# The last two output blocks of the second feed-forward cut at 384 tokens instead of 256

## Chip, cores and metric

One core of a Trainium2 chip runs the whole block, forward pass only, for one sequence of 512 tokens. The metric is the time of one execution in device microseconds; three timed runs of the kernel before and one profiled execution are at hand.

## What is computed

The input x is 512 tokens of 1024 channels. The block has a first feed-forward, a token mixer (an mLSTM branch and a gated delta-net branch, with gates and an output projection), a second feed-forward and a last RMS norm. The change is in the second feed-forward and the norm behind it:

```python
def swiglu(h, w_in, w_out):
    gate, up = jnp.split(h @ w_in, 2, axis=-1)
    return (jax.nn.silu(gate) * up) @ w_out
...
        h = modulate(rms_norm(x, norm_ffn2[l]), mod[:, 2, 0], mod[:, 2, 1])
        x = x + FFN_RES * mod[:, 2, 2][:, None, :] * swiglu(h, w_ffn2_in[l], w_ffn2_out[l])
    return rms_norm(x, norm_final)
```

D_MODEL is 1024 (eight tiles of 128 channels, KO = 8), D_FF is 2816 (22 tiles of 128, in two halves of HJ = 11). All inputs are float32.

## The kernel before

Activations lie with channels on the 128 partitions and tokens along the free axis, so a tile of 128 channels is 128x512. Every large product is made of three matmuls: weights and activations are each split into a rounded high part and a rest (`whi`, `wlo`; `acth`, `actl`; all of the type fp32r), and `mm3` adds high times high, high times low and low times high into one PSUM bank. The weights are the stationary operand (128 columns), the activations the moving one. Small products, those of the norm among them, are plain float32 and appear in the trace as two records each.

`ffn` (the second one is called in the last line of the kernel's main function, L1303) works in two halves of the hidden tiles. Behind each half come the output blocks: `out_block(o, ...)` multiplies 11 weight tiles with 11 hidden tiles into one bank, 33 matmuls, then VectorE adds the result to x (L388), and in the second half ScalarE squares x (L295, tile `sq`, for the last block `sqlast`) and VectorE sums the squares over the blocks (L297, `sqacc`). In the second half the blocks 0 to 5 are done for all 512 tokens. The last two, 6 and 7, are done in two token ranges: both blocks for the first range, then `norm` for that range, then both for the second range, then `norm` for it. Their two weight tiles are held for both ranges.

For the second feed-forward, `norm` is `final` (L1293). It calls `rms_bcast`: per group of 128 tokens, a product of `sqacc` and one of `sqlast` with a column of ones gives the sums over channels (tile `psm`), VectorE makes the mean square (L306, L309), GpSimd raises it to the power -1/2 (L312, `rr`), and one product per group of 128 tokens spreads it over the partitions (`psm<-cstt,rr`). ScalarE scales x by the norm's weight (L1297), and VectorE multiplies by the spread value, two channel tiles at a time (L1299); behind each such step SyncE issues a DMA of the two tiles to HBM (L1301), four per token range.

The order on each engine is set by a scheduler from the order of the program, so that matmuls of the second range stand between the steps of the first range's norm. The queues themselves are served in order. `pbig` is the bank of an output block (three of them in turn).

Of the kernel before, what the change touches and what calls it, by code (L numbers as in the profile page):

```python
# [17 lines left out]
P = 128  # L18
S = 512
TB = S // P  # L20
# [145 lines left out]
def hybrid_block(ctx: ExitStack, tc: tile.TileContext, I, outT, dbg=None, upto=99):  # L166
# [13 lines left out]
    def big():  # L180
        b = ps.tile([P, S], F32, tag="big", name="pbig", bufs=3)
        return b

    def st2():
        b = ps.tile([P, S], F32, tag="st", name="pst", bufs=2)
        return b

    def sm():
        b = ps.tile([P, S], F32, tag="sm", name="psm", bufs=3)
        return b  # L190
# [9 lines left out]
    x = p1.tile([P, KO, S], F32, name="x")  # L200
# [23 lines left out]
    def wtile(src, n=2048, lo=vec):  # L224
        raw = wraw(src, n)
        hi = W.tile([P, 2048], F32R, tag="whi", name="whi")
        wl = W.tile([P, 2048], F32R, tag="wlo", name="wlo")
        for c in range(0, n, 1024):
            e = slice(c, min(n, c + 1024))
            act.activation(hi[:, e], raw[:, e], AF.Copy)  # L230
            lo.tensor_tensor(out=wl[:, e], in0=raw[:, e], in1=hi[:, e].bitcast(F32), op=ALU.subtract)  # L231
        return hi, wl

    def wk(src, c=256, lo=vec):
        hi, lo = wtile(src, KO * c, lo)
        return (hi[:, :KO * c].rearrange("p (k c) -> p k c", c=c),
                lo[:, :KO * c].rearrange("p (k c) -> p k c", c=c))

    def mm3(o, wh, wl, xh, xl, n=KO):
        for k in range(n):  # L240
            mm(o, wh(k), xh(k), start=(k == 0), stop=False)
            mm(o, wh(k), xl(k), start=False, stop=False)
            mm(o, wl(k), xh(k), start=False, stop=(k == n - 1))
# [4 lines left out]
    ghalf = cst.tile([P, 16], F32, name="ghalf")  # L248
# [39 lines left out]
    ALL = (slice(0, S), range(TB))  # L288
    HALVES = ((slice(0, S // 2), range(TB // 2)), (slice(S // 2, S), range(TB // 2, TB)))

    def sumsq(x, k, sq, tp, c=ALL[0], fold=False):
        if c.start == 0:
            tag = "sqacc" if k == 0 else "sqlast" if k == KO - 1 else "sq"
            sq[k] = tp.tile([P, S], F32, tag=tag, name=tag, bufs=2 if tag == "sq" else 1)
        act.activation(sq[k][:, c], x[:, k, c], AF.Square)  # L295
        if 0 < k < (KO if fold else KO - 1):
            vec.tensor_tensor(out=sq[0][:, c], in0=sq[0][:, c], in1=sq[k][:, c], op=ALU.add)  # L297
# [20 lines left out]
    def new_h():  # L318
        hh = Hp.tile([P, KO, S], F32R, tag="hh", name="hh")
        hl = Hp.tile([P, KO, S], F32R, tag="hl", name="hl")  # L320
        return hh, hl

    def split(dst_h, dst_l, src):
        act.activation(dst_h, src, AF.Copy)
        vec.tensor_tensor(out=dst_l, in0=src, in1=dst_h.bitcast(F32), op=ALU.subtract)
# [19 lines left out]
        return f  # L345


    def ffn(x, hh, hl, gcol, wi, wo, tp, norm, side=(), pre=(), first=(ALL,), store=None):
        side, pre = list(side), list(pre)
        sq = {}  # L350
        for half in range(2):
            ah, al = [], []
            for jj in range(HJ):
                j = half * HJ + jj
                if j == 0 and not pre:
                    w0 = [wk(wi[i]) for i in range(2)]
                    p0 = [(big(), big()), (st2(), st2())]
                    for c, _ in first:
                        for (wh, wl), pp in zip(w0, p0):
                            for o, c0 in zip(pp, (0, P)):  # L360
                                mm3(o[:, c], lambda k: wh[:, k, c0:c0 + P], lambda k: wl[:, k, c0:c0 + P],
                                    lambda k: hh[:, k, c], lambda k: hl[:, k, c])
                if j < len(pre):
                    pg, pu = pre[j]
                elif j < 2:
                    pg, pu = p0[j]
                else:
                    wh, wl = wk(wi[j - len(pre)])
                    pg, pu = big(), big()
                    for o, c0 in ((pg, 0), (pu, P)):  # L370
                        mm3(o, lambda k: wh[:, k, c0:c0 + P], lambda k: wl[:, k, c0:c0 + P],
                            lambda k: hh[:, k], lambda k: hl[:, k])
                sg = tp.tile([P, S], F32, tag="sg", name="sg", bufs=2)
                act.activation(sg, pg, AF.Silu)  # L374
                vec.tensor_tensor(out=sg, in0=sg, in1=pu, op=ALU.mult)  # L375
                a_h = tp.tile([P, S], F32R, tag="acth", name="acth", bufs=HJ + 2)
                a_l = tp.tile([P, S], F32R, tag="actl", name="actl", bufs=HJ + 2)
                split(a_h, a_l, sg)
                ah.append(a_h)
                al.append(a_l)  # L380
                if side and j > 1:
                    side.pop(0)()

            def out_block(o, wh, wl, c):
                po = big()
                mm3(po[:, c], lambda k: wh[:, k * P:(k + 1) * P], lambda k: wl[:, k * P:(k + 1) * P],
                    lambda k: ah[k][:, c], lambda k: al[k][:, c], n=HJ)
                vec.scalar_tensor_tensor(out=x[:, o, c], in0=po[:, c], scalar=gcol[:, o:o + 1], in1=x[:, o, c],  # L388
                                         op0=ALU.mult, op1=ALU.add)
                if half == 1:  # L390
                    sumsq(x, o, sq, tp, c)
                    if store is not None and c.stop == S:
                        nc.sync.dma_start(store[:, o], x[:, o])

            for o in range(KO - 2 * half):
                out_block(o, *wtile(wo[o, half], HJ * P), ALL[0])
                if half == 0 and side:
                    side.pop(0)()
        w2 = [wtile(wo[o, 1], HJ * P) for o in (KO - 2, KO - 1)]
        for c, ts in HALVES:  # L400
            for o, w in zip((KO - 2, KO - 1), w2):
                out_block(o, *w, c)
            norm(sq, c, ts)
        assert not side, len(side)
# [38 lines left out]
    hh, hl = new_h()  # L443
    pre = [(big(), big()), (big(), st2()), (st2(), sm()), (sm(), sm())]
    for k in range(KO):
# [36 lines left out]
    negm = cst.tile([P, 2, P], BF16, name="negm")  # L482
    hm = []
    ffn(x, hh, hl, ghalf[:, 0:8], I["wi1"], I["wo1"], pa1, norm_mod(x, 1, hm, p1),
        [lambda b=b, q=q: ada(b, q, pa1) for b in (2, 4, 3, 5, 7, 6, 8) for q in range(4)], pre, store=xd)
    hh, hl = hm
# [144 lines left out]
    for t in range(TB):  # L631
        ts = slice(t * P, (t + 1) * P)
# [16 lines left out]
    for t in range(TB - 1, -1, -1):  # L649
        ts = slice(t * P, (t + 1) * P)  # L650
# [75 lines left out]
    for h in range(H):  # L726
        wh, wl = wk(I["wmqk"][h])
        qk = []
        for i in range(2):
            pq = big()  # L730
            c = slice(i * P, (i + 1) * P)
# [17 lines left out]
        for t in range(TB):  # L749
            ts = slice(t * P, (t + 1) * P)  # L750
# [18 lines left out]
        for t in range(TB):  # L769
            ts = slice(t * P, (t + 1) * P)  # L770
# [39 lines left out]
    for h2 in range(4):  # L810
        wh, wl = wk(I["wmo"][h2])
        for i in range(2):
            h = h2 * 2 + i
            c = slice(i * P, (i + 1) * P)
# [66 lines left out]
    for h in range(H):  # L881
        if h % 2 == 0:
            wvh, wvl = wk(I["wgv"][h // 2])
            for i in range(2):
                c = slice(i * P, (i + 1) * P)
# [7 lines left out]
        for i in range(2):  # L893
            c = slice(i * P, (i + 1) * P)
# [33 lines left out]
        for d in range(2):  # L928
# [4 lines left out]
            for t in range(TB):  # L933
                for hf in range(2):
                    c = slice(t * P + hf * 64, t * P + hf * 64 + 64)
# [3 lines left out]
        for c2 in range(2):  # L939
            pk = st2()  # L940
            for cc in range(2):
                t = c2 * 2 + cc
                ts = slice(t * P, (t + 1) * P)
# [221 lines left out]
    for pr in range(H // 2):  # L1165
        hs = (2 * pr, 2 * pr + 1)
        L = {}
        for h in hs:
            tp = g3c if pr % 2 else g3a
# [9 lines left out]
        for n in range(TB):  # L1179
            rrs, banks = {}, {}  # L1180
            for ci, (h, d) in enumerate(chains):
                vt, X, kd, kq, A, xst, ost = L[h]
                t = n if d == 0 else TB - 1 - n
                ts = slice(t * P, (t + 1) * P)
# [17 lines left out]
            for h, d in chains:  # L1202
                vt, X, kd, kq, A, xst, ost = L[h]
                t = n if d == 0 else TB - 1 - n
                ts = slice(t * P, (t + 1) * P)
# [62 lines left out]
    x = px.tile([P, KO, S], F32, name="x2")  # L1268
    nc.sync.dma_start(x, xd)
    hm = []  # L1270
# [20 lines left out]
    p2 = Lines(ctx.enter_context(tc.tile_pool(name="p2", bufs=1)))  # L1291

    def final(sq, c, ts):  # L1293
# [4 lines left out]
        for k in range(0, KO, 2):  # L1298
            vec.tensor_tensor(out=x[:, k:k + 2, c], in0=x[:, k:k + 2, c],  # L1299
                              in1=rb[:, c].unsqueeze(1).to_broadcast([P, 2, n]), op=ALU.mult)  # L1300
            nc.sync.dma_start(outT[:, k:k + 2, c], x[:, k:k + 2, c])  # L1301

    ffn(x, hm[0], hm[1], ghalf[:, 8:16], I["wi2"], I["wo2"], p2, final, first=HALVES)  # L1303


# [17 lines left out]
```

## Time and profile before

| what | value |
|---|---|
| timed runs | 1569.15, 1570.06, 1571.91 us (median 1570.06) |
| profiled execution, its own time | 1564.87 us |
| its span in the trace | 1563.1 us |
| mean granted TensorE clock | 0.995 |
| TensorE matmul busy | 1529.7 us, 98% of the span |
| VectorE, ScalarE busy | 860.5 us (55%), 731.1 us (47%) |

The profiled execution lies 5.2 us below the median of the timed runs, and its span 1.8 us below its own time. Matmuls are pipelined and their ends are modelled, so the cadence of a matmul is read from the starts of many in a row and not from its duration.

### The profile page before, as it was taken

The numbers are of one execution on the slowest core, as the hardware profiler recorded it, in microseconds if no ns is written. First come the engines' busy times: TensorE is split into PE (matmuls) and PEld (weight loads), VectorE is DVE, ScalarE is ACT, GpSimd is POOL, SyncE is SP. The second block draws the span as 40 slices with busy tenths as digits, with TensorE's granted clock in tenths as the row PEclk, the third lists the DMA queues.
The fourth block names the chain that finished last, engine by engine and source line by source line (L and its number), as shares of the span: only waits on it lengthen the run. The fifth ranks groups of instructions, "written<-read, shape, count | busy, mean of one in ns | idle before, by whom it ended". The sixth has DMA issues, their size and how long they took to land.

```text
span 1563.1 us, 20823 instructions
## 1 busy us (share of the span) xinstructions
PE 1529.7 (98%) x7920; PEld 1288.6 (82%) x7920; DVE 860.5 (55%) x1577; ACT 731.1 (47%) x1654; POOL 54.7 (4%) x88
## 2 busy tenths in 40 slices
PE   8999999999999999989999999989999999999997
PEld 6888888888788888768888887879889888888887
DVE  7897843335735555657677683347556323332333
ACT  4422223223447757886666536757434322222232
POOL 0000000000000000021121200000000000000000
PEclk9999999999999999999999999999999999999999
DMA  9687832233332231364565766675531322323222
GB/s 362 224 335 281 299 139 96 75 113 113 116 133 95 81 95 55 121 212 173 188 205 174 257 243 196 194 290 173 192 136 55 110 98 74 110 108 108 70 88 73
DMA packets 75014, 244.50 MB, mean 156 GB/s; under 512 B 23937, under 2 KB 26369, under 8 KB 58402
## 3 DMA queue, kind: packets, MB, share of 16 engines
q1 hardware_dynamic: 74914, 243.17, 44.7%
q8 instruction: 62, 1.02, 0.3%
q14 instruction: 38, 0.31, 0.1%
HBM read 207.43 MB, written 35.72 MB: 156 GB/s over the span
## 4 chain that ended last, share of the span: by engine, by line
PE 92%; ACT 3%; DVE 2%; DMA 2%; issue 1%; SPq 0%; POOL 0%; POOLq 0%; DVEq 0%; ACTq 0%
PE pbig L193 76%; PE pst L193 8%; PE psm L193 7%; DMA L<-grd 1%; DMA kd<-kdd 0%; PE pst L876 0%; ACT L L936 0%; ACT whi L230 0%; DMA xtd<-X 0%; PE pst L1158 0%; PE pst L909 0%; DVE cmx L645 0%; PE pst L747 0%; ACT L936 0%; PE psm L823 0%
## 5 line engine op out<-in xcount | busy, mean ns | idle before, releaser
L193 PE MATMUL pbig<-hh,whi 128*128 128x512 f32 (+1 forms) x1304 | 509.4, 392 | 7.2 <-ACT whi L230 5.6
L193 PE MATMUL pbig<-hl,whi 128*128 128x512 f32 (+1 forms) x1304 | 507.6, 390 | 0.0
L193 PE MATMUL pbig<-hh,wlo 128*128 128x512 f32 (+1 forms) x1304 | 507.6, 390 | 0.0
L230 ACT ACTIVATE whi<-raw 128x1024 fp32r<-128x1024 f32 (+1 forms) x249 | 237.1, 985 | 421.4 <-PE pbig L193 349.9
L231 DVE TENSOR_TENSOR wlo<-raw,whi 128x1024 fp32r<-128x1024 f32 (+1 forms) x249 | 278.3, 1137 | 99.1 <-ACT whi L230 94.2
L193 PEld LDWEIGHTS pbig<-hh,whi 128*128 128x128 f32 x1304 | 245.5, 189 | 54.3 <-ACT whi L230 5.8
L193 PEld LDWEIGHTS pbig<-hh,wlo 128*128 128x128 f32 x1304 | 245.8, 189 | 49.3 <-DVE wlo L231 1.1
L193 PEld LDWEIGHTS pbig<-hl,whi 128*128 128x128 f32 x1304 | 246.0, 189 | 47.9
L375 DVE TENSOR_TENSOR sg<-sg,pbig 128x512 f32<-128x512 f32 x40 | 27.5, 688 | 233.7 <-PE pbig L193 233.7
L193 PE MATMUL pbig<-acth,whi 128*128 128x512 f32 (+1 forms) x396 | 145.2, 367 | 0.0
L193 PE MATMUL pbig<-acth,wlo 128*128 128x512 f32 (+1 forms) x396 | 144.7, 365 | 0.0
L193 PE MATMUL pbig<-actl,whi 128*128 128x512 f32 (+1 forms) x396 | 144.7, 365 | 0.0
L193 PEld LDWEIGHTS pbig<-actl,whi 128*128 128x128 f32 x396 | 74.7, 189 | 12.1
L193 PEld LDWEIGHTS pbig<-acth,whi 128*128 128x128 f32 x396 | 74.7, 189 | 12.1
L193 PEld LDWEIGHTS pbig<-acth,wlo 128*128 128x128 f32 x396 | 74.6, 188 | 12.1
L374 ACT ACTIVATE sg<-pbig 128x512 f32<-128x512 f32 x41 | 24.6, 599 | 124.2 <-PE pbig L193 123.0
L869 DVE SCALAR_TENSOR_TENSOR cacc<-pbig,cols,cacc 128x510 f32<-128x510 f32 (+1 forms) x96 | 71.5, 747 | 20.0 <-ACT cacc L864 18.5
L388 DVE SCALAR_TENSOR_TENSOR x<-pbig,ghalf,x 128x512 f32<-128x512 f32 (+1 forms) x36 | 24.9, 690 | 99.3 <-PE pbig L193 99.3
L264 DVE SCALAR_TENSOR_TENSOR adaw<-adaw,cs 128x1024 f32<-128x1024 f32 x56 | 66.9, 1221 | 17.1 <-DMA adaw<-in_wada 17.1
L924 POOL TENSOR_SCALAR kd<-tt,ckd 128x128 f32<-128x128 f32 x64 | 43.3, 695 | 234.5 <-DVE ckd L920 193.0
L312 POOL TENSOR_TENSOR rr<-ms,mhalf 128x2 f32<-128x2 f32 x6 | 4.2, 696 | 1054.7 <-DVE ms L309 758.8
L334 ACT ACTIVATE hh<-xr,modc 128x256 fp32r<-128x256 f32 (+1 forms) x40 | 20.5, 545 | 34.5 <-DVE xr L330 34.5
(346 smaller groups left out, 1990.5 us busy)
## 6 DMA issues: line engine op xcount, KB each, us to landing
raw<-in_wi SPq DMA_DIRECT2D x40, 1024.0 KB, 4.8
adaw<-in_wada SPq DMA_DIRECT2D x28, 1024.0 KB, 5.8
raw<-in_wo SPq DMA_DIRECT2D x32, 704.0 KB, 4.1
adaw<-in_wada SPq DMA_DIRECT2D x16, 512.0 KB, 10.2
raw<-in_wmqk SPq DMA_DIRECT2D x8, 1024.0 KB, 4.9
raw<-in_wgkq SPq DMA_DIRECT2D x8, 1024.0 KB
tad<-TA SPq DMA_DIRECT2D x8, 1024.0 KB, 5.9
raw<-in_wis SPq DMA_DIRECT2D x8, 512.0 KB, 8.6
```

Source lines behind the costliest of these rows:

```text
L193: pe.matmul(o, l, r, start=start, stop=stop)
L230: act.activation(hi[:, e], raw[:, e], AF.Copy)
L231: lo.tensor_tensor(out=wl[:, e], in0=raw[:, e], in1=hi[:, e].bitcast(F32), op=ALU.subtract)
L264: vec.scalar_tensor_tensor(out=raw[:, n], in0=raw[:, n], scalar=1.0, in1=cs, op0=ALU.mult, op1=ALU.mult, accum_out=acc[:, n:n + 1])
L312: pool.tensor_tensor(out=r, in0=ms, in1=mhalf.to_broadcast([P, n]), op=ALU.pow)
L334: act.activation(hh[:, k, c], xr, AF.Identity, bias=b)
L374: act.activation(sg, pg, AF.Silu)
L375: vec.tensor_tensor(out=sg, in0=sg, in1=pu, op=ALU.mult)
L388: vec.scalar_tensor_tensor(out=x[:, o, c], in0=po[:, c], scalar=gcol[:, o:o + 1], in1=x[:, o, c], op0=ALU.mult, op1=ALU.add)
L869: vec.scalar_tensor_tensor(out=acc[:, o], in0=pz[:, i], scalar=w[:, j:j + 1], in1=acc[:, o], op0=ALU.mult, op1=ALU.add)
L924: pool.tensor_scalar(out=kd[:, d, t], in0=ktt[:, t], scalar1=ckd[:, t, d, h:h + 1], scalar2=None, op0=ALU.mult)
```

## The change

The token ranges of the last two output blocks become a parameter of `ffn`, with the two halves as its default. The second feed-forward passes tokens 0 to 383 (three groups of 128) and tokens 384 to 511 (one group). The first feed-forward keeps the halves.

```diff
-    def ffn(x, hh, hl, gcol, wi, wo, tp, norm, side=(), pre=(), first=(ALL,), store=None):
+    def ffn(x, hh, hl, gcol, wi, wo, tp, norm, side=(), pre=(), first=(ALL,), store=None, last=HALVES):
...
         w2 = [wtile(wo[o, 1], HJ * P) for o in (KO - 2, KO - 1)]
-        for c, ts in HALVES:
+        for c, ts in last:
             for o, w in zip((KO - 2, KO - 1), w2):
                 out_block(o, *w, c)
             norm(sq, c, ts)
...
-    ffn(x, hm[0], hm[1], ghalf[:, 8:16], I["wi2"], I["wo2"], p2, final, first=HALVES)
+    ffn(x, hm[0], hm[1], ghalf[:, 8:16], I["wi2"], I["wo2"], p2, final, first=HALVES,
+        last=((slice(0, 3 * P), range(3)), (slice(3 * P, S), range(3, TB))))
```

## Rows read from the trace of the kernel before

**Rows 1.** The page: the span, and the chain that ended last, by engine.

```profile
span 1563.1 us, 20823 instructions
PE 92%; ACT 3%; DVE 2%; DMA 2%; issue 1%; SPq 0%; POOL 0%; POOLq 0%; DVEq 0%; ACTq 0%
```

**Rows 2.** Windows: range 1, range 2, and the end behind the last matmul.

```profile
core 0: us, PE busy (x) PEld busy (x) DVE busy (x) ACT busy (x) POOL busy (x), PEclk, DMA share, GB/s
1535.30:1543.15 7.85, 7.85 (x67) 7.85 (x66) 3.96 (x6) 3.79 (x7) 0.00 (x0) 1.00 0.01 2
1543.15:1553.40 10.25, 9.71 (x83) 9.51 (x81) 4.10 (x9) 1.86 (x4) 0.69 (x1) 1.00 0.31 102
1553.40:1563.10 9.70, 1.65 (x11) 1.29 (x11) 3.28 (x7) 0.92 (x2) 0.69 (x1) 0.71 0.32 108
```

**Rows 3.** Timeline (start, us): first matmul of two full blocks, first and last of range 1.

```profile
1520.32 0.39 PE L193 MATMUL pbig<-acth,whi 128*128 128x512 f32 x1
1527.80 0.39 PE L193 MATMUL pbig<-acth,whi 128*128 128x512 f32 x1
...
1535.28 0.28 PE L193 MATMUL pbig<-acth,whi 128*128 128x256 f32 x1
...
1543.07 0.28 PE L193 MATMUL pbig<-acth,wlo 128*128 128x256 f32 x1
```

**Rows 4.** Timeline, plain float32 records in a row: weight loads (PEld) and matmuls (PE).

```profile
1037.92 1.64 PEld L193 LDWEIGHTS psm<-xs,A 128*128 128x128 f32 x14
416.03 1.86 PEld L193 LDWEIGHTS psm<-gg,cgt 128*128 128x128 f32 x16
414.69 0.34 PE L193 MATMUL psm<-cgt,lf 128*8 128x2 f32 x8
418.70 1.91 PE L193 MATMUL psm<-cgt,gg 128*8 128x128 f32 x16
```

**Rows 5.** Timeline, inside range 2: the norm of range 1.

```profile
1545.76 0.28 PE L193 MATMUL pbig<-acth,wlo 128*128 128x256 f32 x1
1546.57 0.52 PEld L193 LDWEIGHTS psm<-cstt,rr 128*128 128x128 f32 x4 [0.74 <-POOL rr L312]
1547.32 2.48 DVE L1299 TENSOR_TENSOR x<-x,psm 128x512 f32<-128x512 f32 x4 [1.71 <-PE psm L193]
```

**Rows 6.** Timeline, behind the last matmul.

```profile
1553.43 0.48 DVE L388 SCALAR_TENSOR_TENSOR x<-pbig,ghalf,x 128x256 f32<-128x256 f32 x1 [2.32 <-PE pbig L193]
1553.95 0.42 ACT L295 ACTIVATE sqlast<-x 128x256 f32<-128x256 f32 x1 [2.75 <-DVE x L388]
1554.41 0.52 PEld L193 LDWEIGHTS psm<-cstt,sqlast 128*128 128x128 f32 x4 [0.77 <-ACT sqlast L295]
1555.49 0.69 POOL L312 TENSOR_TENSOR rr<-ms,mhalf 128x2 f32<-128x2 f32 x1 [8.97 <-DVE ms L309]
1556.98 2.48 DVE L1299 TENSOR_TENSOR x<-x,psm 128x512 f32<-128x512 f32 x4 [1.57 <-PE psm L193]
1557.70 2.16 SPq L1301 DMA_DIRECT2D out_dram<-x  x4
```

**Rows 7.** Groups by line and shape: VectorE and ScalarE steps of other widths (busy us, mean ns).

```profile
L1193 DVE SCALAR_TENSOR_TENSOR rr<-psm,neggam,vt 128x128 f32<-128x128 f32 x24 | 7.8, 345 | 1.7 <-PE psm L193 1.6
L231 DVE TENSOR_TENSOR wlo<-raw,whi 128x1024 fp32r<-128x1024 f32 x30 | 35.8, 1223 | 2.2 <-ACT whi L230 0.3
L297 DVE TENSOR_TENSOR sqacc<-sqacc,sq 128x256 f32<-128x256 f32 x6 | 2.5, 424 | 2.1 <-ACT sq L295 2.1
L1142 ACT ACTIVATE jk<-ost 128x128 bf16<-128x128 f32 x32 | 9.9, 308 | 7.0 <-DVE ost L1138 6.4
```

**Rows 8.** DMA view of 1555.1 to 1563.1 us (0.2 us a slice); then 1038.0 to 1039.8.

```profile
DMA  0000000000000000049999999999999980000000
DMA packets 1088, 1.05 MB, mean 131 GB/s; under 512 B 64, under 2 KB 1088, under 8 KB 1088
DMA packets 225, 0.75 MB, mean 416 GB/s; under 512 B 25, under 2 KB 25, under 8 KB 225
```

## The prediction

> **What bounds the kernel now.** I read the page first: TensorE carries 92% of the chain that ended last [rows 1], so what adds matmul time anywhere adds it to the end. The windows over the last 28 us then show three stretches [rows 2]. Range 1 (blocks 6 and 7, tokens 0 to 255) is 7.85 us of unbroken TensorE work. Range 2 is the same matmuls with the norm of range 1 between them, 10.25 us with TensorE busy for 9.71. Behind the last matmul come 9.7 us in which TensorE works for 1.65: the norm of range 2 and its store, one short step after another. The change makes range 1 wider and range 2 and that last stretch narrower. The granted clock is 1.00 in both matmul stretches, and the 0.71 of the last one has almost nothing to slow.
>
> **What a matmul costs by its width.** Starts give the cadence [rows 3]. A full block is 33 matmuls of 512 columns in 1527.80 - 1520.32 = 7.48 us, 0.2267 us each. Range 1 is 66 matmuls of 256 columns; first to last start is 65 steps in 1543.07 - 1535.28 = 7.79 us, 0.1198 us each. The difference over 256 columns is 0.000417 us a column, one column per cycle of 2.4 GHz, and 0.013 us is left per matmul at either width. So 384 columns cost 0.1733 us, halfway between.
>
> At 128 columns the trace has no fp32r matmul, and this is the disputed price. The columns alone would be 128 x 0.000417 + 0.013 = 0.067 us. But each matmul loads new weights of 128 columns, and rows show what that costs when the matmul is too short to hide it [rows 4]: 16 records with only 32 moving columns load weights at (1.86 - 0.19)/15 = 0.111 us each, 14 records with 128 columns at (1.64 - 0.19)/13 = 0.112 (0.19 is one load). With weights of only 8 columns and 2 moving ones a record takes (0.34 - 0.16)/7 = 0.026, so it is the 128-column load and not a fixed cost of issuing. These rows are plain float32; that fp32r loads are no slower than 0.120 follows from range 1, where one hides under each matmul. So 0.111 to 0.120 us if loads bind; I take 0.113. The two outer bounds are 0.067 (the load somehow hidden) and the full float32 price, two records of 0.111 = 0.223.
>
> The Trainium skill, "TensorE: Matmul & The Clock Gate", section "Back-to-back issue gap", gives about 81 ns per matmul for a stream of load and matmul pairs at 128 columns. Rows 4 show 0.111 for such pairs, so the trace speaks against it for 4-byte weights; by the page the 66 matmuls would take an estimated 5.3 us instead of 7.5.
>
> **The change part by part.** I sum from the profiled execution, 1564.87 us; it lies 5.2 below the median of 1570.06, and I put the same difference on the median.
>
> Range 1: 66 matmuls go from 0.1198 to 0.1733: **+3.5 us**, with nothing to hide it, as the stretch is unbroken.
>
> Range 2: 66 matmuls go from 0.1198 to 0.113: -0.45. The norm of range 1 now serves three groups of tokens instead of two, each with two records in each of its three products: 18 records instead of 12, 6 x 0.113 = +0.7. TensorE also waits for the GpSimd power in there: its last matmul ends at 1546.04 and the spread starts at 1546.57, 0.53 us [rows 5]. What leads to that power gets about 0.45 us longer (wider VectorE and ScalarE steps, 0.13 and 0.10, and two more `sqlast` records), and the work in between (15 matmuls, 8 records before and 12 after) gets 0.35 longer. So the wait grows by 0.1. It depends on how many matmuls the scheduler puts there: between no wait (-0.5) and 1.0 more. Range 2 together: **+0.35 us**.
>
> VectorE's queue is the next thing that could be late there. Its four multiplies of range 1 (0.683 each, 2.48 in a row [rows 5]) become 768 elements wide, 0.95 each by the 512- and 1024-element rows [rows 5, 7], some 3.6 us in a row. Block 6's addition stands behind them. They start 4.0 us after range 1 ends, 4.6 after the change, and end at 8.2; addition, square and sum add about 1.1, so 9.3, while the matmuls of range 2 end about 10.4 after range 1. It stays hidden, with 1.1 us to spare.
>
> The end [rows 6, 7]: the addition falls from 0.48 to 0.345 (a step of that form at 128 elements), -0.13; the square from 0.42 to 0.308, -0.11; `sqlast` and the spread each lose two records of 0.111, -0.44. The power keeps its 0.69 us (two elements per partition now; I give one nothing). The four multiplies of 256 instead of 512 elements take 0.424 instead of 0.683, so the first store is issued 0.26 earlier and the issues, now 0.72 us and then three more over 2.16 us, can follow each other at about 0.4. The data run from about 1558.5 to 1561.7 at full DMA load in 1088 packets [rows 8]. If a packet costs as much at half the size, only the 0.26 is won; if bytes alone count, the transfer is 1.6 instead of 3.2 us and the end comes 1.8 earlier, then held by the issues. The rates of the 1 KB packets (about 340 GB/s while busy) and of the larger ones (416 GB/s, 3.3 KB on the mean) give about 11 ns per packet and 0.036 ns per byte, 29 ns for 512 bytes against 46 now: 1.5 us earlier, which I take, with 0.3 and 1.8 as bounds. The end together: **-2.2 us** (-1.0 to -2.5).
>
> **Sum:** 3.5 + 0.35 - 2.2 = +1.65 us. The profiled execution would be near 1566.5, the median 1570.06 + 1.65 = **1571.7 us**. With the bounds of the parts (load 0.111 to 0.120: -0.1 to +0.5; wait: -0.6 to +0.9; end: -0.3 to +1.2), each bad end alone and the worst two together reach +4.2, the good ones +0.6. A difference of 0.2%, 3.1 us, is about what a measurement of this kernel can tell from no change, so this is "no change" most likely, on the slow side. The reason in one sentence: a 128-column matmul costs almost what a 256-column one does, so cutting 128 tokens off the last range saves next to nothing there, while the other range pays for them in full.
>
> **Rivals.**
>
> *The 128-column fp32r matmul runs at the full float32 price.* Then 66 x (0.223 - 0.113) = +7.3 us in range 2, less the wait of 0.6 that the longer filling would cover: +8.3 in all, 1578.4 us, slower by 0.5%. For it: no row of this kernel has an fp32r matmul below 256 columns, and all its products of 128 columns are plain float32, so nothing shows that one pass holds there. Against it: 256 and 512 columns both run at one column per cycle with one record each, and nothing in the slope hints at a step. Four cycles a column would give 0.213 + 0.013 = 0.227, much the same. It decides from 0.136 us per matmul on (3.1 - 1.65 = 1.5 us over 66). The Trainium skill, "FP8 and Floating Point Precision", section "TensorE Precision Notes", tells true FP32 (four passes) from a reduced form that is truncated, and ties neither to a width. The plain records agree with four passes (0.107 for 128 columns, twice per product), and no row shows the width.
>
> *The loads hide and 0.067 holds.* Range 2's matmuls would take 4.4 us, 3.0 less than in my sum. But then VectorE's queue becomes the bound: the last addition can't start before about 9.3 us after range 1, so about 1.2 of the 3.0 arrive: +0.4, 1570.5 us. If the scheduler lets block 6's addition pass the multiplies, -1.2, 1568.9. Against it: rows 4. Even then it is not faster by a measurable amount, since 384 and 128 columns together cost as much as twice 256 and the end gives only 2.2.
>
> *The store's end doesn't move*, being bound by packets: -0.3 instead of -1.5 there, +2.85, 1572.9 us. It lies within my own case.
>
> **How the numbers follow.** My case 0.60, the float32 price 0.25, hidden loads 0.12, something unseen 0.03. My case alone spans 1570.7 to 1574.3. To leave out no more than 2 in 10 the range must reach the float32 price with a poor end, 1580.5, and it goes down to 1568.5 below hidden loads. My case is slower by over 0.2% with 0.17 of its weight and faster with 0.02; the float32 price is slower. That makes slower 0.36, same 0.60, faster 0.04.
>
> **What would show it.** In the profile after: 384-column matmuls start every 0.173 us and range 1 lasts 11.4 us; the 128-column starts are 0.111 to 0.120 apart, with weight loads back to back (two records per product, or over 0.2 between starts, for the float32 price; 0.07 for hidden loads). Range 2 lasts about 10.4 us, with six records per product of the norm; the stretch from the last matmul's end to the end of the span shrinks from 9.7 to about 7.5, most of it between the first and the last store. I am wrong if the 128-column step lies outside 0.10 to 0.136, if the scheduler moves the first norm so that TensorE waits over 1.5 us, or if VectorE's multiplies hold block 6.

## The result and the profile after

The changed kernel took 1578.03 us (median of 4 executions, 1574.19 to 1581.63) against 1569.61 us of the kernel before in the same series; the ratio is 1.0061 with a 95% interval of 1.0045 to 1.0078. It is slower by 7 to 12 us, beyond the 0.2% that can be told from no change. The profiled execution took 1574.19 us.

Windows of the changed kernel: range 1 (384 columns), range 2 up to 1553.8 us, the rest of range 2, and the end.

```profile
1536.89:1548.51 11.62, 11.62 (x70) 11.62 (x68) 4.22 (x6) 4.02 (x7) 0.00 (x0) 1.00 0.01 1
1548.51:1553.80 5.29, 4.17 (x37) 3.90 (x36) 1.64 (x4) 1.14 (x2) 0.85 (x1) 1.00 0.00 0
1553.80:1564.33 10.53, 10.53 (x52) 10.53 (x51) 3.49 (x6) 0.71 (x2) 0.00 (x0) 0.50 0.41 149
1564.33:1572.40 8.07, 1.72 (x7) 1.25 (x6) 2.08 (x7) 0.71 (x2) 0.55 (x1) 0.50 0.23 65
```

These answer to [rows 2]. Look at the granted clock, the third number from the end: 1.00 (2.4 GHz) in the first two, 0.50 (1.2 GHz) from 1553.8 on, in the middle of range 2. In the kernel before it was 1.00 to the end of the matmuls. The timeline shows the moment, matmuls and weight loads:

```profile
1553.41 0.28 PE L193 MATMUL pbig<-acth,wlo 128*128 128x128 f32 x1
1553.52 0.28 PE L193 MATMUL pbig<-acth,whi 128*128 128x128 f32 x1
1553.63 0.27 PE L193 MATMUL pbig<-actl,whi 128*128 128x128 f32 x1
...
1553.90 0.41 PE L193 MATMUL pbig<-acth,whi 128*128 128x128 f32 x1
1554.11 0.41 PE L193 MATMUL pbig<-actl,whi 128*128 128x128 f32 x1
...
1563.92 0.41 PE L193 MATMUL pbig<-acth,wlo 128*128 128x128 f32 x1
```

```profile
1553.46 0.19 PEld L193 LDWEIGHTS pbig<-acth,whi 128*128 128x128 f32 x1
1553.57 0.19 PEld L193 LDWEIGHTS pbig<-actl,whi 128*128 128x128 f32 x1
...
1553.80 0.33 PEld L193 LDWEIGHTS pbig<-acth,whi 128*128 128x128 f32 x1
1554.00 0.33 PEld L193 LDWEIGHTS pbig<-actl,whi 128*128 128x128 f32 x1
```

Up to there a 128-column matmul starts every 0.11 us, and each load takes 0.19 us, as the prediction had it from the plain float32 rows [rows 4]. Then load and matmul slow down together: from 1553.90 to 1563.92 there are 47 steps of 0.213 us. Each product is one record throughout, so the two-record price of plain float32 is not what happened. What stood before the fall, in the timeline of the norm of range 1:

```profile
1549.78 0.83 PE L193 MATMUL psm<-cstt,sqlast 128*128 128x1 f32 x6
1551.23 0.85 POOL L312 TENSOR_TENSOR rr<-ms,mhalf 128x3 f32<-128x3 f32 x1 [353.85 <-DVE ms L309]
1552.13 0.93 PE L193 MATMUL psm<-cstt,rr 128*128 128x128 f32 x6 [1.12 <-POOL rr L312]
```

TensorE waited 1.12 us for the power, twice as long as before [rows 5]: the scheduler put 9 matmuls of range 2 ahead of the spread, where the kernel before had 15.

The same kernel profiled again (run e8 below, 1571.01 us) has no fall before the last matmul: range 1, range 2, the end.

```profile
1538.83:1550.45 11.62, 11.62 (x70) 11.62 (x68) 4.22 (x6) 4.03 (x7) 0.00 (x0) 1.00 0.01 1
1550.45:1561.32 10.87, 9.74 (x87) 9.48 (x85) 5.04 (x9) 1.85 (x4) 0.85 (x1) 1.00 0.40 144
1561.32:1569.20 7.88, 1.35 (x7) 0.88 (x5) 2.08 (x7) 0.71 (x2) 0.55 (x1) 0.60 0.24 67
```

So one kernel shows the split with and without the fall. From the first matmul of range 1 to the end of the span (before: 1535.28, 1543.35, 1553.40 and 1563.10 are the borders):

| stage, us | before | changed, no fall | changed, fall | forecast of the difference |
|---|---|---|---|---|
| range 1 | 8.07 | 11.62 | 11.62 | +3.5 |
| range 2 | 10.05 | 10.87 | 15.82 | +0.35 |
| end | 9.70 | 7.88 | 8.07 | -2.2 |
| together | 27.82 | 30.37 (+2.55) | 35.51 (+7.69) | +1.65 |

The fall costs 15.82 - 10.87 = 4.95 us in range 2, and 47 steps x (0.213 - 0.112) = 4.8 is nearly all of it.

The times of whole executions hold more than these stages. Up to range 1 all the kernels run the same code, and yet range 1 began 1.6 us later in the first profile, 3.5 us later in e8 and 5.6 us later in e9 than in the kernel before; over all profiles of this case it began between 1535.05 us (e4) and 1540.92 us (e9). Part of that is half clock elsewhere: from 950 to 960 us e9 has a mean granted clock of 0.83, the kernel before 1.00. So two executions are compared by their stages, and of the 14 us by which e9's profiled execution (1578.79 us) is above that of the kernel before, 5.6 stand ahead of everything that was changed.

### The profile page after: what moved, and what is told of

It is laid out like the page before. It is cut to its first block, busy times and chain, and to the rows that moved or that the text cites. A ratio compares the mean times of both kernels' runs of the same rounds, so it can differ in the third digit from the quotient of the medians.

```text
span 1572.4 us, 20823 instructions
## 1 busy us (share of the span) xinstructions
PE 1538.5 (98%) x7920; PEld 1297.3 (83%) x7920; DVE 859.8 (55%) x1577; ACT 730.7 (46%) x1654; POOL 54.4 (3%) x88
## 4 chain that ended last, share of the span: by engine, by line
PE 91%; ACT 3%; DVE 2%; DMA 2%; issue 1%; SPq 0%; POOL 0%; POOLq 0%; DVEq 0%; ACTq 0%
PE pbig L193 74%; PE pst L193 8%; PE psm L193 7%; DMA L<-grd 1%; PE pst L876 0%; DMA kd<-kdd 0%; DMA vt<-vtd 0%; ACT L L936 0%; ACT whi L230 0%; PE pst L909 0%; DVE cacc L869 0%; PE pst L1158 0%; DVE cmx L645 0%; PE pst L747 0%; ACT L871 0%
## 5 line engine op out<-in xcount | busy, mean ns | idle before, releaser
L193 PE MATMUL pbig<-acth,whi 128*128 128x512 f32 (+3 forms) x396 | 148.2, 374 | 0.0
L193 PE MATMUL pbig<-acth,wlo 128*128 128x512 f32 (+3 forms) x396 | 148.0, 374 | 0.0
L193 PE MATMUL pbig<-actl,whi 128*128 128x512 f32 (+3 forms) x396 | 147.9, 373 | 0.0
L388 DVE SCALAR_TENSOR_TENSOR x<-pbig,ghalf,x 128x512 f32<-128x512 f32 (+3 forms) x36 | 24.8, 690 | 107.0 <-PE pbig L193 107.0
L312 POOL TENSOR_TENSOR rr<-ms,mhalf 128x2 f32<-128x2 f32 (+2 forms) x6 | 4.2, 705 | 1064.1 <-DVE ms L309 767.5
## 6 DMA issues: line engine op xcount, KB each, us to landing
adaw<-in_wada SPq DMA_DIRECT2D x16, 512.0 KB, 10.5
```

The source lines that it names most:

```text
L193: pe.matmul(o, l, r, start=start, stop=stop)
L312: pool.tensor_tensor(out=r, in0=ms, in1=mhalf.to_broadcast([P, n]), op=ALU.pow)
```

## The experiments

Two theories stand at the start. "Columns": a run of 128-column matmuls makes the clock fall by itself. "Wait": the 1.12 us that TensorE waits for the power starts it. The ratios below are against the kernel before in the same series.

**256 columns, 128 used (e3).**

```diff
-                mm3(po[:, c], ...
+                m = slice(S - 256, S) if c.start == 3 * P else c
+                mm3(po[:, m], ...
```

> The 384/128 split, but the matmuls of the second range run over tokens 256 to 511 (256 columns); only the last 128 columns are used, the norm and the store are those of the 384/128 split. 66 x 0.120 = 7.9 us instead of 7.4 at full clock. Both theories: the clock stays at 1.00 to the last matmul. If the clock alone makes the changed kernel slow, more columns make it faster: +3.5 (range 1) +0.8 (norm records, wait) -2.2 (end) = +2 against the kernel before, some 1571.7, and 5 to 8 us faster than the changed kernel. If something else in the split costs it, it stays at +8.

Measured: 1570.06 us, ratio 1.0016 (1.0005 to 1.0028), and 1.00 to the last matmul. Windows of range 1, range 2, end:

```profile
1536.76:1548.39 11.63, 11.63 (x70) 11.62 (x68) 4.22 (x6) 4.03 (x7) 0.00 (x0) 1.00 0.01 1
1548.39:1559.25 10.86, 10.16 (x87) 9.96 (x85) 5.04 (x9) 1.85 (x4) 0.85 (x1) 1.00 0.37 132
1559.25:1566.80 7.55, 0.99 (x7) 0.63 (x5) 2.08 (x7) 0.71 (x2) 0.55 (x1) 0.84 0.30 88
```

Twice the columns per matmul make range 2 five microseconds shorter than in the profile with the fall (10.86 against 15.82). Everything else of the split is still in this kernel, and together it costs 30.04 - 27.82 = +2.2 us by the windows, +2.5 by the ratio. So of the changed kernel's loss (0.61% is 9.6 us) some 2.5 us are the split's, and what is left went away when its narrow matmuls got wider and kept the clock: 7 us by the ratios, 35.51 - 30.04 = 5.5 us by the windows of the two profiles. The rest of the 7 is in no window that was compared. The wait shrank too, to 0.70 us, so this run alone does not tell columns from wait.

**A longer wait between 256-column matmuls (e4).** The kernel before, with this in the first norm of the last pair of ranges:

```diff
+            pool.tensor_tensor(out=r, in0=r, in1=one1.to_broadcast([P, n]), op=ALU.mult)
```

> The kernel before (256/256) with one more GpSimd step of about 0.7 us in the first norm of the last range pair (a multiplication of the power's result by one), so that TensorE waits about 1.2 us inside range 2 instead of 0.53, as long as in the changed kernel. Theory 'wait': the clock falls to 0.50 behind it and the remaining 256-column matmuls cost 0.213 or more; slower by 4 us and more. Theory 'columns': the clock stays at 1.00 to the last matmul, and the time is that of the kernel before plus 0.7 at most: same.

Measured: 1566.09 us, ratio 0.9998 (0.9983 to 1.0013). The wait grew less than expected, since the added step took only 0.2 us and the scheduler put one more matmul ahead:

```profile
1546.61 0.71 PE L193 MATMUL psm<-cstt,rr 128*128 128x128 f32 x4 [0.69 <-POOL rr L314]
...
1543.12:1553.31 10.19, 9.50 (x82) 9.30 (x80) 4.10 (x9) 1.85 (x4) 0.88 (x2) 1.00 0.31 103
```

0.69 instead of 0.53 us of wait, and the clock stayed at 1.00. That is no test of 1.1 us; but the 256-wide run above had 0.70 with all of the changed kernel's norm records and also kept it.

**Narrow matmuls in one piece (e1).** Both norms moved behind all matmuls of the second feed-forward; the first one, which keeps `HALVES`, stays as it is.

```diff
             for o, w in zip((KO - 2, KO - 1), w2):
                 out_block(o, *w, c)
-            norm(sq, c, ts)
+            if last is HALVES:
+                norm(sq, c, ts)
+        if last is not HALVES:
+            for c, ts in last:
+                norm(sq, c, ts)
```

> The 384/128 split, but both norms stand behind all matmuls, so the 66 matmuls of 128 columns run in one piece, with no norm product and no wait for GpSimd between them. Theory 'columns' (a run of 128-column matmuls, bound by weight loads, makes the granted clock fall to 0.50 by itself, and each then takes 0.213 us instead of 0.111): the clock still falls inside this run, and most starts from there are 0.213 apart; range 2 lasts well over 7.3 us. Theory 'wait' (the 1.1 us in which TensorE waits for the power of the first norm starts the fall): the clock stays at 1.00 through range 2 and 66 x 0.111 = 7.3 us. The stretch behind the last matmul grows by some 4 us, as it now holds the first norm too, so the time is no judge: by 'columns' about 1580 or more, by 'wait' about 1575.

Measured: 1573.56 us, ratio 1.0039 (1.0027 to 1.0051). Windows of range 2 and of the end:

```profile
1552.20:1559.78 7.58, 7.58 (x70) 7.58 (x68) 1.26 (x3) 1.85 (x4) 0.00 (x0) 1.00 0.00 0
1559.78:1574.40 14.62, 4.38 (x25) 3.91 (x23) 5.86 (x13) 0.71 (x2) 1.40 (x2) 0.57 0.42 143
```

1.00 through all 66, starts 0.1117 apart: "columns" did not happen here. From range 1 to the end of the span it is 33.56 us against 27.82 before, and most of that is the end of 14.6 us, which now holds both norms: 4.9 us more than the 9.70 before, where I expected some 4.

**128 tokens first (e2).** `last=((slice(0, P), range(1)), (slice(P, S), range(1, TB)))`.

> The split turned round: tokens 0 to 127 first, then 128 to 511. The 128-column matmuls now follow directly on the 512-column blocks. Theory 'columns': the clock falls inside range 1 or soon behind it, although TensorE has waited for nothing before; it comes back among the 384-column matmuls. Theory 'wait': 1.00 throughout range 1, 66 x 0.111 = 7.3 us, and any fall comes only behind the wait for the power. Range 2 takes 11.4 us at full clock, the end is longer than before (three groups of tokens, 768-element multiplies, 1.5 times the store): about +2. By 'wait' about 1575, by 'columns' 1576 to 1581.

Measured: 1573.34 us, ratio 1.0045 (1.0029 to 1.0061). The profiled execution (1570.11 us) kept 1.00 through both ranges:

```profile
1535.23:1542.70 7.47, 7.47 (x69) 7.46 (x67) 3.69 (x6) 3.59 (x7) 0.00 (x0) 1.00 0.01 2
1542.70:1555.57 12.87, 12.47 (x76) 12.15 (x74) 3.26 (x9) 1.86 (x4) 0.55 (x1) 1.00 0.14 41
1555.57:1568.30 12.73, 3.05 (x19) 2.58 (x17) 4.49 (x7) 1.14 (x2) 0.87 (x1) 0.63 0.34 124
```

As "wait" had it. But four of its ten executions took 1576.9 to 1579.5 us, and I have no trace of one of those, so it doesn't clear narrow matmuls altogether.

"Columns" alone had failed in e1. "Wait" alone had not been tested, since no wait of 1.1 us between wider matmuls had come about. The theory for the next runs is "both": narrow matmuls hold the clock by themselves, and a wait among them (with the one-column records of the norm) tips it.

**The narrow matmuls twice (e6).** As e1, with each 128-column block multiplied twice into its bank, so the work of range 2 is done twice.

```diff
-                mm3(po[:, c], ...
+                for _ in range(2 if c.start == 3 * P else 1):
+                    mm3(po[:, c], ...
```

> Norms behind all matmuls as before, and each of the two 128-column blocks is multiplied twice into the same bank (the first product is overwritten), so 132 matmuls of 128 columns run in one piece, 14.7 us at 0.111. Theory 'both': no wait and no one-column records inside, so the clock stays at 1.00 to the last of them. Rival 'columns, only slow' (128-column matmuls alone do it, and 7.4 us were too short): the clock falls inside the run, after more than 7.4 us of it, and the rest costs 0.213 each.

Measured, one execution: 1577.85 us. Window of range 2:

```profile
1546.50:1561.40 14.90, 14.90 (x136) 14.90 (x134) 1.26 (x3) 1.85 (x4) 0.00 (x0) 1.00 0.00 1
```

132 narrow matmuls in a row, 14.9 us, at 1.00. "Columns, only slow" falls, for this execution.

**The changed kernel without the wait (e7, and again as e10).** The same instructions; the norm of range 1 is cut into three steps, and `out_block` calls them between its matmuls:

```diff
+                steps = norm(sq, c, ts)
+                next(steps)
...
+                out_block(KO - 2, *w2[0], c, {3: lambda: next(steps), HJ - 1: lambda: next(steps, None)})
+                out_block(KO - 1, *w2[1], c)
```

> The changed kernel with the first norm's products put where nothing waits for them: sqacc at the start of range 2, sqlast behind 12 matmuls of block 6, the spread behind all 33 of block 6. The same instructions, the wait of 1.1 us gone. Theory 'both': without the wait the clock stays at 1.00, range 2 is 66 x 0.111 + 18 x 0.111 = 9.4 us, and the time is some 1 us above the kernel before: same. If narrow matmuls and the one-column records are enough without the wait, it falls here too and the time is +7 to +8.

> The changed kernel without the wait again. So far nine of ten executions lay at 0.994 to 0.996 and one at 0.988. Theory 'both': at most two in ten at 0.991 or below, 1.000 to 1.002 against the kernel before, and clearly below the changed kernel. If the wait is not what tips it, the counts are alike.

Measured: ratio 1.0009 (0.9992 to 1.0026), the second time 1.0017 (0.9997 to 1.0037). Range 2 in the first profile:

```profile
1549.07:1558.40 9.33, 9.33 (x85) 9.19 (x83) 4.89 (x9) 1.85 (x4) 0.85 (x1) 1.00 0.18 65
```

No wait, 1.00, 9.33 us (9.4 expected); 1.00 and 9.41 us in the second profile. It gives back most of the loss. But not in every execution: four of the 22 show a mean granted clock of 0.988 or 0.989 and take 1573.3 to 1580.5 us, three of them among the 12 of e10, a little more than the two in ten expected. Without the wait such executions are rarer, not gone. The one-column records of the norm are still among the narrow matmuls here, at other places, so they and the narrow matmuls are mostly not enough without the wait.

**192 columns, 128 used (e5).** As e3 with `slice(S - 192, S)`.

> As the changed kernel, but the matmuls of the second range run over 192 columns (tokens 320 to 511), of which the last 128 are used. The weight loads still bind, so a matmul should cost 0.111 to 0.120 us at full clock, as with 128 columns, and the wait for the power inside range 2 is at least as long as in the changed kernel. By now neither theory holds alone: 128 columns in one piece kept 1.00 for 7.4 us (norms last), and a longer wait between 256-column matmuls kept it too. Theory 'both' (narrow matmuls leave so little in reserve that the wait and the norm's one-column records tip it): with half as many columns again the clock stays at 1.00 and the time is that of the 256-wide run, +2 to +3 against the kernel before. Rival 'wait behind load-bound matmuls' (what counts is that loads bind, and the wait; the columns don't matter): it falls as in the changed kernel, +8.

Measured: 1572.6 us, ratio 1.0031 (1.0019 to 1.0043). The profiled execution kept 1.00 in range 2, 11.24 us with a wait of 1.21 us:

```profile
1550.50:1561.74 11.24, 9.86 (x87) 9.52 (x85) 5.04 (x9) 1.85 (x4) 0.85 (x1) 1.00 0.39 140
```

The starts are 0.1117 apart, where 192 columns alone would take 0.093 by the prediction's price of a column, so loads bind at 192 columns too. Three of ten executions lie at 0.991 and 1573.6 to 1577.2 us, the others at 0.993 to 0.995. That is no clear sign of a fall, since the kernel before in the same series has three of 19 at 0.991. So the wait among load-bound matmuls is mostly not enough when they have 192 columns: this speaks against "wait" alone and against "wait behind load-bound matmuls", and "both" stands. Its forecast of the time (+2 to +3 us) was low; the ratio says +3 to +7.

**The changed kernel again (e8, e9).**

> The changed kernel once more, to see at which point of range 2 the clock falls in another execution, and its time beside the other runs on the same chip. All theories: slower by 0.5 to 0.7%, starts of 0.213 us from some point of range 2 on. If that point lies elsewhere than 5 us into range 2, the spread of its times (1574 to 1582) is explained by it: each matmul at the lower clock costs 0.10 more.

> The changed kernel on the same chip as the one without the wait, in as many executions, to count how often the clock falls inside range 2. So far seven of eight executions of it had a mean granted clock of 0.988 to 0.991 (the profiled one with the fall 0.991), one 0.993 (the profiled one without a fall). Theory 'both' (the wait and the one-column records tip a stretch of narrow matmuls that holds by itself): most executions at 0.991 or below, 1.005 to 1.007 against the kernel before.

Measured: e8 1577.23 us, ratio 1.0055 (1.0036 to 1.0074), and its profiled execution the one without a fall that is shown above, against every theory's expectation of it. e9 1578.66 us, ratio 1.0059 (1.0040 to 1.0078); there the fall comes again, at the first matmuls behind the spread:

```profile
1552.54:1557.20 4.66, 3.53 (x31) 3.27 (x30) 1.00 (x4) 1.14 (x2) 0.85 (x1) 1.00 0.00 0
1557.20:1568.94 11.74, 11.74 (x58) 11.74 (x57) 4.13 (x6) 0.71 (x2) 0.00 (x0) 0.50 0.38 134
```

Counting executions by their mean granted clock (0.991 in the first profile with the fall, 0.988 in the second, 0.993 in the one without):

| kernel | columns in range 2 | wait in range 2, us | at 0.991 or below | at 0.990 or below |
|---|---|---|---|---|
| changed | 128 | 1.12 | 17 of 20 | 16 of 20 |
| changed, 192 wide | 192 | 1.21 | 3 of 10 | 0 of 10 |
| changed, no wait | 128 | 0 | 4 of 22 | 4 of 22 |
| changed, 256 wide | 256 | 0.70 | 0 of 12 | 0 of 12 |
| before, longer wait (e4) | 256 | 0.69 | 0 of 10 | 0 of 10 |
| before, no wait (e11) | 256 | 0 | 0 of 12 | 0 of 12 |
| before | 256 | 0.53 | 4 of 83 | 0 of 83 |

The mean runs over the whole execution, and the kernel before has short stretches at half clock elsewhere too, so the count is a sign of a fall in range 2 and not a record of one; the last row is what it shows without any change. e1, e2 and e6 are left out because their longer ends, largely at half clock, lower the mean: e6's one execution has 0.991 with 1.00 all through range 2.

**Halves without the wait (e11).** The form of e7 with ranges of 256 and 256.

> The kernel before (256/256) with the first norm's products at the same places as in the kernel without the wait. It is the version that the parts point to: no wider range 1, no wait. The wait of 0.53 us goes, 1.0 us at most with the changeovers. All theories: the clock stays at 1.00, 0.9995 to 1.000 against the kernel before, so no difference that can be measured, and 1 to 2 us faster than the 384/128 form without the wait.

Measured: 1565.55 us against 1567.66, ratio 0.9986 (0.9973 to 0.9999). Range 2 takes 9.24 us at 1.00 instead of 10.05:

```profile
1547.37:1556.61 9.24, 9.24 (x82) 9.24 (x80) 4.06 (x9) 1.85 (x4) 0.69 (x1) 1.00 0.25 84
```

The 0.8 us saved there is shown. The 2.1 us between the medians is more than the profile accounts for, and the interval of the ratio reaches to 0.2 us.

## Why the prediction was right or wrong

The range (1568.5 to 1580.5 us) held the time. The case it called likeliest, no change at 1571.7 us, did not come, and the time lies near the 1578.4 of a rival whose mechanism did not happen. That the range held it is luck. By a sign that the prediction named itself it was wrong: the 128-column step left 0.10 to 0.136 us, with 0.213. The step that failed is in the first paragraph: "The granted clock is 1.00 in both matmul stretches, and the 0.71 of the last one has almost nothing to slow." I read the clock of the kernel before as that of the kernel after and gave no chance to a range 2 that runs at half clock. The runs showed 0.50 for 10.53 of its 15.82 us in the first profile and for 11.74 of 16.40 us in e9, which costs 4.95 and 5.5 us against the execution without the fall.

- *Range 1, +3.5 us:* right. 65 steps of 0.1737 us (0.1733 forecast), 11.62 us instead of 8.07.
- *The 128-column matmul is bound by its load, 0.111 to 0.120 us:* right at full clock. 0.1117 in e1, e6 and e7. 192 columns cost the same (e5). The load goes with the granted clock, 0.213 at half, and so the price I had taken from full-clock rows did not hold.
- *The Trainium skill's 81 ns* ("TensorE: Matmul & The Clock Gate", "Back-to-back issue gap") did not appear: 0.1117, as [rows 4] had it.
- *Range 2, +0.35 us:* mis-sized. Without the fall it grew by 0.82. The wait was forecast to grow by 0.1 and grew by 0.6. What leads to the spread grew much as forecast (from the last matmul's end of range 1 to the spread 3.22 us before, 3.62 after), though the power of three elements took 0.85 us instead of 0.69. What failed is TensorE's work in between: 0.35 us more was forecast, and it was 0.19 less (2.69 and 2.50 us), because the scheduler placed 9 matmuls before the spread instead of 15.
- *VectorE's queue stays hidden:* right in the changed kernel. In e7, where its multiplies start later, block 7's addition starts at 1558.47, behind them, 0.07 us after the last matmul's end.
- *The end, -2.2 us:* -1.8 without the fall, -1.6 with it. The power, "I give one nothing", took 0.55 us instead of 0.69. The spread, forecast 0.22 shorter, got 0.09 longer in e8 (0.74 us to the first multiply before, 0.83 after): its two records run at a granted clock of 0.50 there, the four of the kernel before took 0.71 us. From the first multiply to the end of the span it is 4.81 us instead of 6.12, 1.3 won instead of the 1.5 taken: the DMA view of the end in e8 shows data over some 11 slices of 0.2 us, 2.2 us, where the 29 ns per packet that I worked out give 1.9 us for 1024 packets on 16 engines.

```profile
1563.56 0.80 PE L193 MATMUL psm<-cstt,rr 128*128 128x128 f32 x2 [1.07 <-POOL rr L312]
1564.39 1.41 DVE L1299 TENSOR_TENSOR x<-x,psm 128x256 f32<-128x256 f32 x4 [1.52 <-PE psm L193]
...
DMA  0000000000000000000000697996988950000000
DMA packets 1099, 0.53 MB, mean 66 GB/s; under 512 B 72, under 2 KB 1099, under 8 KB 1099
```

- *The sum:* the range of my own case was added wrongly. The worst two ends, 1.2 and 0.9, reach 1.65 + 2.1 = +3.75 us; the +4.2 takes all three.
- *The rivals:* the float32 price is refuted by the single records at 0.1117; its 8.3 us agreed with the measurement by chance, since half clock doubles a load-bound step just as two records would. Hidden loads never occurred.

Shown: the clock's fall costs 4.95 us in the first profile (table of stages), 256 columns in the same place, with a wait of 0.70 us, avoid it (e3), taking out the wait avoids it in most executions (e7, e10), 192 columns with a wait of 1.21 us avoid it in most too (e5), and neither 66 nor 132 narrow matmuls in one piece brought it on in the profiled executions (e1, e6). So in the runs made here it needed the 128-column matmuls, and in most executions the wait as well. Still open: what exactly in range 2 tips it. A wait among 128-column matmuls without the one-column records was not run, a wait of 1.1 us between 256-column matmuls was not run (e4 reached 0.69), and why three of 20 executions of the changed kernel escape and four of 22 without the wait don't is not seen in any trace. The executions above 1579 us, up to 1584.6, have no trace either; a late start of range 1, as in e9, may be part of them.

## What to carry to other kernels

A matmul whose weight load takes longer than its moving columns saves no time by being narrower (192 and 128 columns both 0.112 us, 256 columns 0.120 us), so a narrow last range pays for the wider one before it and gets back only what the steps behind it lose. Before narrowing, ask of each stretch whether its granted clock would survive: here the narrow stretch held 1.00 in one piece in every profile and mostly lost it with a wait of 1.1 us inside. Filling the wait was worth more than the split: it saves 0.8 us of range 2 with 256 and 256 (e11), where the split costs 2.2 to 2.5 us without any fall. The ratio of that form, 0.9986, is the lowest of those run here, by an interval that only just ends below 1.

## What the hardware showed that I had not expected

- The granted clock fell to 0.50 in the middle of a stretch in which TensorE then stayed busy without a gap, and it did not rise again in 10.5 us of back-to-back 128-column matmuls (11.7 us in e9).
- A weight load of 128 columns slows with the granted clock: 0.19 to 0.33 us for one, 0.112 to 0.213 us from start to start.
- The GpSimd power takes 0.55, 0.69 and 0.85 us for one, two and three elements per partition; I had taken it as fixed.
